# A decoder block with 32 experts on one core: gate and up products per matrix in four column groups, and another order at the end

## The chip, the cores and the metric

The kernel runs on 1 core of a Trainium2 chip. The metric is the device time of one execution in microseconds; the time before is 1613.85 us, the median of 3 runs (1612.68 to 1614.62).

## The reference, cut to what matters

One decoder layer over 256 tokens of width 2048, float32: RMS norm, an input projection, two attention branches (8 heads each), gates, an output projection; then a mixture of experts and a final RMS norm. The change lies in the experts and the end:

```
def hier_moe(h, ...):                      # 4 groups of 8 experts, 32 in all
    # each token: the best group, in it the two best experts, and their weights
    ...
    yb = (silu(xblk @ w_gate[e]) * (xblk @ w_up[e])) @ w_down[e]      # 2048 -> 512 -> 2048
    out[token] += yb * weight
x = x + hier_moe(rms_norm(x, norm2_g), ...)
return rms_norm(x, norm_f_g)
```

All 32 experts' matrices are read: 96 matrices of 2048 x 512 floats, 4.19 MB each.

## The kernel before

The first 680 us compute attention and projections. The routing then gives each expert up to 32 slots (`CAP`); four experts (a `QUAD`) share a tile of 128 slots. `gather` makes the quad's tokens, transposed, with one-hot products into `xq`. `hidden(e)` multiplies: for each of 16 slices k of the 2048 inputs the 32 slots are the stationary operand (128 x 32) and a row of the matrix is the moving one. The array is used as four column groups of 32 columns, `c` = 0 to 3: two for the gate matrix and two for up, each with 256 of the 512 hidden columns. The hidden columns are dealt out so that `w_down` can be read in long rows: line 723 gives a group neighbouring pairs of floats, every other pair.

```
rhs = (gw, uw)[c // 2][j].rearrange("p (q a b) -> p a q b", a=2, b=2)[:, c % 2]
nc.tensor.matmul(gu[c * CAP:(c + 1) * CAP], lhsT, rhs, start=(k == 0), stop=(k == KT - 1))
```

A float32 product is one instruction in the listings of the program, and two weight loads with two matmuls in the trace. Gate and up go side by side: a slice k of gate, the same of up. After silu, product and two transposes (`hTe`), `expert` multiplies with the down matrix (four column groups of 512 outputs, `py`), copies to `y`, and after four experts `combine` adds the slots to the tokens' rows `x1` with a product with the weighted one-hot matrix `owT` (float32).

The matrices come through a ring of five slots of 4.19 MB (`W`, `G`, `H`, `Q`, `O`), filled by SyncE's queue in the order of `plan`; a transfer is issued when its slot's last content has been used. At the start of the stage the slots hold gate, up, down 0, gate 1 and then up 1; expert 2's gate and up come in parts of 1 and 2 MB, each into the part of a slot that expert 0 has just used (line 398 and on). From down 2 (the name for expert 2's down matrix) on, whole matrices follow in the order gate, up, down.

At the end gate 31 and up 31 come in halves and quarters and are multiplied side by side, with `keep_clock` products (line 546, results unused) between the quarters. Down 31 comes in five column blocks, `BLOCKS`, on SyncE's queue; block by block: `last_down`, a copy, `combine` with `owl`, the squares for the norm. `norm_out` scales and writes eight blocks on SyncE's queue. The order of instructions on each engine is set by a scheduler that goes by data dependences and its own estimates, so it differs in places from the order of the code.

Of the kernel before, what the change touches and what calls it, by code (L numbers as in the profile page):

```python
# [9 lines left out]
F32 = mybir.dt.float32  # L10
F32R = mybir.dt.float32r
# [3 lines left out]
OP = mybir.AluOpType  # L15
# [17 lines left out]
BIG = 1e30  # L33
CH = 512
ROUTING_WAIT = 4
LOAD_WAIT = 2
BLOCKS = ((0, 512), (512, 512), (1024, 512), (1536, 256), (1792, 256))


@with_exitstack  # L40
def decoder_block(ctx, tc, x, g1T, w_in, b_gates, w_out_m, w_out_d, w_o, g2T, g2r, wr, br,
# [25 lines left out]
    def at(shape, name="at"):  # L67
        return psum.tile(shape, F32, tag="at", name=name, bufs=2)
# [336 lines left out]
    tags = [again[(len(rest) + i) % 5] for i in range(4)]  # L405
    for lo, hi in ((0, 8), (8, 12), (12, 16)):
        plan += [(kind, NE - 1, lo, hi, tags[i], lo) for i, kind in enumerate("gu")]
    plan_at = [0]

    def ring_part():  # L410
# [296 lines left out]
            k = k0 + j  # L707
            nc.scalar.activation(out=xq[:, k // 8, k % 8], in_=p[:, j], func=AF.Copy, scale=g2p[:, k:k + 1])

    def hidden(e, og=None):  # L710
        s0 = (e % QUAD) * CAP
        gu = at([P, S], name="gu")
        if og:
            gather(og, 0)
            gather(og, 2)
        for half in range(2):
            gw = units("g", e, 8 * half, 8 * half + 8)
            uw = units("u", e, 8 * half, 8 * half + 8)
            for j in range(8):
                k = 8 * half + j  # L720
                lhsT = xq[:, half, j, s0:s0 + CAP]
                for c in range(4):
                    rhs = (gw, uw)[c // 2][j].rearrange("p (q a b) -> p a q b", a=2, b=2)[:, c % 2]
                    nc.tensor.matmul(gu[c * CAP:(c + 1) * CAP], lhsT, rhs, start=(k == 0), stop=(k == KT - 1))  # L724
                if og and j % 4 == 3 and k + 1 < KT:
                    gather(og, k + 1)
                    gather(og, k + 3)
                if e == NE - 1 and j % 4 == 3 and k + 1 < KT:
                    keep_clock(LOAD_WAIT, rows[0][0][:, 0:4])
        sil = t2([P, S], name="sil")  # L730
        nc.scalar.activation(out=sil[64:128], in_=gu[0:64], func=AF.Silu)  # L731
        hh = t2([P, S], name="hh")
        nc.vector.tensor_tensor(out=hh[64:128], in0=gu[64:128], in1=sil[64:128], op=OP.mult)  # L733
        ph = tp([P, 2, 64])
        hv = hh[64:128].rearrange("q (p j) -> q j p", j=2)
        for j in range(2):
            nc.tensor.transpose(ph[:, j], hv[:, j], ident[64:128, 64:128])
        hTe = t2([P, 2, 2, CAP], name="hTe")
        nc.vector.tensor_copy(out=hTe, in_=ph.rearrange("p j (a s) -> p j a s", a=2))  # L739
        return hTe  # L740

    def expert(e, y, og):
        s0 = (e % QUAD) * CAP
        hTe = hidden(e, og)
# [12 lines left out]
        for c in range(4):
            src, dst = py[c * CAP:(c + 1) * CAP], y[c][s0:s0 + CAP]
            if c % 2:
                nc.vector.tensor_copy(out=dst, in_=src)  # L760
            else:
                nc.scalar.copy(out=dst, in_=src)  # L762

    def combine(owT, yc, b0, w):
        cs = slice(b0, b0 + w)
        for t in range(NT):
            p = acc([P, CH], name="pc")[:, 0:w]
            nc.tensor.matmul(p, owT[:, t * P:(t + 1) * P], yc, start=True, stop=True)
            nc.vector.tensor_tensor(out=x1[:, t, cs], in0=p, in1=x1[:, t, cs], op=OP.add)

    for q in range(NQ):
        if q:
            og = onehots(q, False, "og")
        owT = None
        y = []
        for e in range(q * QUAD, (q + 1) * QUAD):
            if e < NE - 1:
                expert(e, y, og if e % QUAD == 0 else None)
            if e % QUAD == 0:
                ows = onehots(q, True, "ow")  # L780
                owT = slots_T(ows)
                if q == NQ - 1:

                    last = []
                    for t in range(NT):
                        o = t2([P, QUAD, CAP], name="ol")
                        nc.vector.tensor_copy(out=o, in_=ows[t][:, P - CAP:].unsqueeze(1).to_broadcast([P, QUAD, CAP]))
                        last.append(o.rearrange("p e s -> p (e s)"))
                    owl = slots_T(last)
            if e == 1:  # L790
                keep_rows()
            if e == min(NE - 2, (q + 1) * QUAD - 1):
                for c in range(4):
                    combine(owT, y[c], c * CH, CH)

    hTe = hidden(NE - 1)
    gfs, gfr = (slot(tags[2])[:, i * D:(i + 1) * D] for i in range(2))
    nc.sync.dma_start(gfr[0:1], gf)
    last_slot = slot(tags[3])
    last_view = w_down[NE - 1].rearrange("(p j) c -> p j c", j=4)  # L800
    last_dw = []
    for b0, w in BLOCKS:
        t = last_slot[:, 4 * b0:4 * (b0 + w)].rearrange("p (j c) -> p j c", j=4)
        nc.sync.dma_start(t, last_view[:, :, b0:b0 + w])
        last_dw.append(t)
    nc.gpsimd.partition_broadcast(gfs, gfr[0:1])
    sf = region("bgs", [P, NT, len(BLOCKS)], name="sf")
    nc.scalar.activation(out=warm, in_=hTe[:, 0, 0, 0:1], func=AF.Sqrt, scale=0.0, bias=one)

    def last_down(b):  # L810
        w = BLOCKS[b][1]
        dw = last_dw[b]
        py = acc([P, CH], name="py")[:, 0:w]
        for i in range(4):
            nc.tensor.matmul(py[i * CAP:(i + 1) * CAP], hTe[:, i % 2, i // 2], dw[:, i],
                             start=True, stop=True)
        yl = t2([P, CH], name="yl")[:, 0:w]
        if b < len(BLOCKS) - 1:
            nc.scalar.copy(out=yl, in_=py)
        else:  # L820
            nc.vector.tensor_copy(out=yl, in_=py)
        return yl

    def square_sums(b):
        b0, w = BLOCKS[b]
        cs = slice(b0, b0 + w)
        for t in range(NT):
            sq = t2([P, CH], name="sq")[:, 0:w]
# [8 lines left out]
    def norm_out():  # L837
        rfs = []
        n = len(BLOCKS) - 1
        most = sm([P, NT], name="most")  # L840
        nc.vector.tensor_reduce(out=most, in_=sf[:, :, 0:n], axis=AX.X, op=OP.add)
        nc.vector.tensor_scalar(most, most, 1.0 / D, EPS, op0=OP.mult, op1=OP.add)
        for t in range(NT):
            mf = sm([P, 1], name="mf")
            nc.scalar.activation(out=mf, in_=sf[:, t, n:n + 1], func=AF.Sqrt, scale=1.0 / D, bias=most[:, t:t + 1])
            rf = sm([P, 1], name="rf")
            nc.vector.reciprocal(rf, mf)
            rfs.append(rf)
        for t in range(NT):
            rf = rfs[t]  # L850
            for c in range(4):
                cs = slice(c * CH, (c + 1) * CH)
                if c == 3:
                    nc.vector.scalar_tensor_tensor(out=xg[t][:, cs], in0=x1[:, t, cs], scalar=rf, in1=gfs[:, cs],
                                                   op0=OP.mult, op1=OP.mult)
                elif t == 0:
                    nc.vector.tensor_scalar(xg[t][:, cs], xg[t][:, cs], rf, None, op0=OP.mult)
                else:
                    nc.scalar.activation(out=xg[t][:, cs], in_=xg[t][:, cs], func=AF.Copy, scale=rf)
                nc.sync.dma_start(out[t * P:(t + 1) * P, cs], xg[t][:, cs])  # L860
# [105 lines left out]
```

## Time and profile before

| | us |
|---|---|
| median of 3 runs | 1613.85 |
| the profiled execution | 1615.2 |
| its span | 1613.5 |
| TensorE busy (matmul) | 1275.5 |
| VectorE busy | 570.9 |
| ScalarE busy | 482.8 |

528.3 MB move in all, 327 GB/s over the span. The profile's clock figure is the share of TensorE's full clock that was granted: 0.891 over the whole. Line numbers are those of the kernel before, unless they stand in the change. "DMA share" is the mean busy share of the core's 16 DMA engines. In the chain of the execution that ended last, TensorE has 59% and DMA 36%, of which 35% is waiting for up matrices. "PEld" is a weight load of TensorE, "PE" a matmul.

### The profile page before, as it was taken

What the parts mean: (1) busy time and instruction counts of PE and PEld (TensorE: products, weight loads), DVE (VectorE), ACT (ScalarE), POOL (GpSimd) and SP (SyncE); (2) the same over time, 40 slices, a digit from 0 to 9 for tenths busy, and PEclk for the clock granted to TensorE, in tenths of its full rate; (3) what the DMA queues carried; (4) which work ended last, traced back from release to release, by engine and by line L of the source; (5) the groups of instructions that cost most, each with busy time, mean ns of one, the idle gap of its engine ahead of it and who ended that gap; (6) DMA issues with size and microseconds to landing.
All of it is one profiled execution on the core that took longest, in us unless ns stands there. A gap on an engine that the chain in (4) does not pass through costs nothing.

```text
span 1613.5 us, 22882 instructions
## 1 busy us (share of the span) xinstructions
PE 1275.5 (79%) x9531; PEld 875.1 (54%) x9532; DVE 570.9 (35%) x1078; ACT 482.8 (30%) x1004; POOL 132.3 (8%) x159
## 2 busy tenths in 40 slices
PE   8999999999999999995846755666656757647666
PEld 7888888888888878762422322322323323314322
DVE  5766666666666665511200200201102112102122
ACT  6555555565656554420100100101100101001003
POOL 0200001013223130001000000000000000000001
PEclk9999999999999999997968877878877878877878
DMA  8544454485545578699999999999999999999994
GB/s 288 191 160 172 160 206 157 157 317 205 201 166 207 193 239 283 239 378 430 430 429 432 431 431 430 430 432 428 431 430 434 431 430 428 430 432 431 432 417 150
DMA packets 82002, 528.30 MB, mean 327 GB/s; under 512 B 4706, under 2 KB 5986, under 8 KB 66914
## 3 DMA queue, kind: packets, MB, share of 16 engines
q1 hardware_dynamic: 80882, 526.41, 80.8%
q8 instruction: 77, 1.26, 0.3%
q10 hardware_dynamic: 1008, 0.35, 0.1%
q14 instruction: 35, 0.28, 0.0%
HBM read 524.65 MB, written 2.10 MB: 326 GB/s over the span
## 4 chain that ended last, share of the span: by engine, by line
PE 59%; DMA 36%; DVE 2%; ACT 1%; issue 1%; POOL 0%; SPq 0%; ACTq 0%; DVEq 0%
DMA ew<-in_w_up 35%; PE gu L724 11%; PE qk L260 7%; PE g L260 7%; PE py L750 4%; PE g L261 4%; PE qk L261 4%; PE y L260 4%; PE tp L705 2%; PE y L261 2%; PE v L153 2%; PE v L151 2%; PE v L152 2%; PE o L152 1%; PE o L153 1%; PE o L151 1%
## 5 line engine op out<-in xcount | busy, mean ns | idle before, releaser
L724 PE MATMUL gu<-ew,xq 128*32 128x256 f32 x4096 | 311.7, 446 | 262.2 <-DMA ew<-in_w_up 185.0
L724 PEld LDWEIGHTS gu<-ew,xq 128*32 128x32 f32 x4096 | 152.1, 123 | 423.9 <-DMA ew<-in_w_up 200.8
L128 DVE TENSOR_TENSOR S<-raw,S 128x512 fp32r<-128x512 f32 x410 | 303.3, 749 | 192.4 <-ACT S L127 165.2
L127 ACT ACTIVATE S<-raw 128x512 fp32r<-128x512 f32 x410 | 257.6, 631 | 229.2 <-DVE S L128 74.0
L733 DVE TENSOR_TENSOR hh<-gu,sil 64x256 f32<-64x256 f32 x32 | 13.7, 427 | 572.7 <-ACT sil L731 572.7
L260 PE MATMUL qk<-hT,S 128*128 128x512 f32 x512 | 185.8, 406 | 0.0
L260 PE MATMUL g<-hT,S 128*128 128x512 f32 x512 | 181.8, 399 | 0.0
L731 ACT ACTIVATE sil<-gu 64x256 f32<-64x256 f32 x32 | 12.0, 376 | 519.6 <-PE gu L724 519.6
L261 PE MATMUL g<-hT,S 128*128 128x256 f32 x512 | 143.7, 281 | 0.0
L261 PE MATMUL qk<-hT,S 128*128 128x256 f32 x512 | 143.0, 280 | 0.0
L750 PE MATMUL py<-ew,hTe 128*32 128x512 f32 x976 | 121.7, 643 | 5.7 <-DVE hTe L739 5.7
L260 PEld LDWEIGHTS g<-hT,S 128*128 128x128 f32 x512 | 96.2, 188 | 23.4
L260 PEld LDWEIGHTS qk<-hT,S 128*128 128x128 f32 x512 | 96.8, 190 | 21.7 <-DVE hT L169 0.2
L760 DVE COPY y<-py 32x512 f32<-32x512 f32 x62 | 42.7, 689 | 168.6 <-ACT y L762 168.3
L261 PEld LDWEIGHTS qk<-hT,S 128*128 128x128 f32 x512 | 97.2, 190 | 0.8
L261 PEld LDWEIGHTS g<-hT,S 128*128 128x128 f32 x512 | 96.6, 189 | 0.1
L762 ACT COPY y<-py 32x512 f32<-32x512 f32 x62 | 35.7, 576 | 187.3 <-PE py L750 168.5
L260 PE MATMUL y<-oT,S 128*128 128x512 f32 x256 | 90.3, 398 | 0.3 <-ACT S L127 0.3
L261 PE MATMUL y<-oT,S 128*128 128x256 f32 x256 | 71.4, 281 | 0.1
L750 PEld LDWEIGHTS py<-ew,hTe 128*32 128x32 f32 x976 | 30.3, 118 | 74.8 <-issue 65.8
L705 PEld LDWEIGHTS tp<-og,x1p 128*128 128x128 f32 x448 | 58.6, 206 | 21.2 <-issue 13.5
L705 PE MATMUL tp<-og,x1p 128*128 128x128 f32 x448 | 63.2, 299 | 7.9 <-ACT og L640 6.7
(221 smaller groups left out, 1383.0 us busy)
## 6 DMA issues: line engine op xcount, KB each, us to landing
ew<-in_w_gate SPq DMA_DIRECT2D x29, 4096.0 KB, 39.2
ew<-in_w_up SPq DMA_DIRECT2D x29, 4096.0 KB, 42.7
ew<-in_w_down SPq DMA_DIRECT2D x29, 4096.0 KB, 29.8
raw<-in_w_in SPq DMA_DIRECT2D x38, 2048.0 KB, 7.8
ew<-in_w_gate SPq DMA_DIRECT2D x10, 1024.0 KB, 8.5
S2s<-in_w_o SPq DMA_DIRECT2D x38, 256.0 KB, 5.2
ew<-in_w_down SPq DMA_DIRECT2D x9, 1024.0 KB, 7.4
raw<-in_w_out_m SPq DMA_DIRECT2D x4, 2048.0 KB, 8.5
```

The costliest lines, as they stand in the source:

```text
L127: a = nc.scalar.activation(out=hi, in_=raw, func=AF.Copy)
L128: b = nc.vector.tensor_tensor(out=lo, in0=raw, in1=hi.bitcast(F32), op=OP.subtract)
L151: nc.tensor.matmul(a[t], lhs_hi[:, ts_], hi, start=(k == 0), stop=False)
L152: nc.tensor.matmul(a[t], lhs_hi[:, ts_], lo, start=False, stop=False)
L153: nc.tensor.matmul(a[t], lhs_lo[:, ts_], hi, start=False, stop=(k == nk - 1))
L260: nc.tensor.matmul(a[i], hi[:, bs], h2, start=(kk == 0), stop=False)
L261: nc.tensor.matmul(a[i][:, 0], lo[:, bs], h2[:, 0], start=False, stop=(kk == nk - 1))
L705: nc.tensor.matmul(p[:, j], rows[0][t][:, k0 + j], og[t], start=(t == 0), stop=(t == NT - 1))
L724: nc.tensor.matmul(gu[c * CAP:(c + 1) * CAP], lhsT, rhs, start=(k == 0), stop=(k == KT - 1))
L750: nc.tensor.matmul(py[c * CAP:(c + 1) * CAP], hTe[:, j % 2, j // 2], dw[c], start=(j == 0), stop=(j == 3))
L760: nc.vector.tensor_copy(out=dst, in_=src)
L762: nc.scalar.copy(out=dst, in_=src)
```

## The change

Gate and up get a PSUM tile each. Each matrix is multiplied in four column groups of 128 hidden columns, so an expert has 16 x 4 x 2 = 128 products of 128 columns where it had 64 of 256; a group's columns are every fourth float. All of gate comes before up, except in the first expert of a quad, where four slices of each alternate. Silu and product now work on 128 rows x 128 columns, with one transpose. At the end the order of transfers and products is gate 30, up 30, gate 31, down 30, up 31, down 31. Experts 30 and 31 have one-hot matrices of their own, not weighted (`of_one`); their outputs are scaled by the slot weights and split into a rounded part and a rest (`weighted`), and summed with two float32r products. Down 31's first block goes on ScalarE's queue, the rest in two loads on SyncE's; the output is written in four transfers on both queues.

```diff
-LOAD_WAIT = 2
-BLOCKS = ((0, 512), (512, 512), (1024, 512), (1536, 256), (1792, 256))
+LOAD_WAIT = 5
+BLOCKS = ((1536, 512), (0, 512), (512, 512), (1024, 256), (1280, 256))
+LAST_LOADS = ((1536, 512), (0, 1024), (1024, 512))
...
-    rest = [("d", 2)] + [(kind, e) for e in range(3, NE - 1) for kind in "gud"]
+    rest = [("d", 2)] + [(kind, e) for e in range(3, NE - 2) for kind in "gud"]
+    rest += [("g", NE - 2), ("u", NE - 2), ("g", NE - 1), ("d", NE - 2), ("u", NE - 1)]
...
+    def quarters(kind, e, og=None):
+        s0 = (e % QUAD) * CAP
+        p = at([P, P], name="gu")
+        def steps(k0, k1):
+            w = units(kind, e, k0, k1)
+            for k in range(k0, k1):
+                rhs = w[k - k0].rearrange("p (q c) -> p c q", c=4)
+                for c in range(4):
+                    nc.tensor.matmul(p[c * CAP:(c + 1) * CAP], xq[:, k // 8, k % 8, s0:s0 + CAP], rhs[:, c],
+                                     start=(k == 0), stop=(k == KT - 1))
+        return p, steps
...
+        if og:
+            for k in range(0, KT, 4):
+                gather(og, k)
+                gather(og, k + 2)
+                g_steps(k, k + 4)
+                u_steps(k, k + 4)
+        else:
+            g_steps(0, KT)
+            u_steps(0, KT)
...
+    def weighted(p, col, name):
+        w = p.shape[1]
+        hi, lo = (t2([P, CH], F32R, name=name)[:, 0:w] for _ in range(2))
+        nc.scalar.activation(out=hi, in_=p, func=AF.Copy, scale=slot_w[:, col:col + 1])
+        nc.vector.scalar_tensor_tensor(out=lo, in0=p, scalar=slot_w[:, col:col + 1], in1=hi.bitcast(F32),
+                                       op0=OP.mult, op1=OP.subtract)
+        return hi, lo
...
+    ohT30, ohT31 = of_one(NE - 2, 0), of_one(NE - 1, 1)
+    hT30 = hidden(NE - 2)
+    load_last(nc.scalar, *LAST_LOADS[0])
+    (g31, g_steps), (u31, u_steps) = (quarters(kind, NE - 1) for kind in "gu")
+    g_steps(0, KT)
+    keep_clock(LOAD_WAIT, rows[0][0][:, 0:4])
+    y30 = weighted(products(NE - 2, hT30), 0, "y30")
...
+    keep_clock(LOAD_WAIT, rows[0][0][:, 0:4])
+    u_steps(0, KT)
+    gfs, gfr = (slot(tags[1])[:, i * D:(i + 1) * D] for i in range(2))
     nc.sync.dma_start(gfr[0:1], gf)
+    for b0, w in LAST_LOADS[1:]:
+        load_last(nc.sync, b0, w)
+    hTe = activated(g31, u31)
...
+        for t in range(NT):
+            p = acc([P, CH], name="pc")[:, 0:w]
+            for i in range(2):
+                nc.tensor.matmul(p, ohT31[:, t * P:(t + 1) * P], yl[i], start=(i == 0), stop=(i == 1))
+            add_block(p, t, slice(b0, b0 + w))
```

Where the scheduler puts the products, on TensorE at the start of the expert stage, from the third quarter of expert 0 to expert 2. Before (`gu` are gate and up products, L705 gathers, L737 transposes, `py` down products):

```order
L724 MATMUL gu<-ew,xq 32x256 x16
L705 MATMUL tp<-og,x_4910 128x128 x8
L724 MATMUL gu<-ew,xq 32x256 x33
L737 MATMUL tp<-ident,hh 128x64 x2
L724 MATMUL gu<-ew,xq 32x256 x4
L750 MATMUL py<-ew,hTe 32x512 x16
L684 MATMUL tp<-ident,ow 128x128 x2
L724 MATMUL gu<-ew,xq 32x256 x45
L737 MATMUL tp<-ident,hh 128x64 x2
L750 MATMUL py<-ews,hTe 32x512 x8
L750 MATMUL py<-ew,hTe 32x512 x8
L724 MATMUL gu<-ew,xq 32x256 x62
```

After, the same stretch:

```order
L720 MATMUL gu<-ew,xq 32x128 x32
L705 MATMUL tp<-og,x_4910 128x128 x8
L720 MATMUL gu<-ew,xq 32x128 x37
L731 MATMUL tp<-ident,hh 128x128
L720 MATMUL gu<-ew,xq 32x128 x8
L755 MATMUL py<-ew,hTe 32x512 x16
L684 MATMUL tp<-ident,ow 128x128 x2
L720 MATMUL gu<-ew,xq 32x128 x120
L731 MATMUL tp<-ident,hh 128x128
L720 MATMUL gu<-ew,xq 32x128 x8
L755 MATMUL py<-ews,hTe 32x512 x8
L755 MATMUL py<-ew,hTe 32x512 x8
```

In both a few of the next expert's products are drawn ahead of the transposes, and the order of the pieces is the same. What moved is within a piece: an expert's 64 products are 128 of half the width, gate before up.

On TensorE at the end, before, from expert 30's transposes on (`idle` are the keep-clock products, `pc` the slot sums):

```order
L737 MATMUL tp<-ident,hh 128x64 x2
L750 MATMUL py<-ew,hTe 32x512 x16
L768 MATMUL pc<-y,owT 128x512 x8
L724 MATMUL gu<-ew,xq 32x256 x2
L546 MATMUL idle<-x1p,ident 128x512 x2
L724 MATMUL gu<-ew,xq 32x256 x30
L546 MATMUL idle<-x1p,ident 128x512 x2
L724 MATMUL gu<-ew,xq 32x256 x16
L546 MATMUL idle<-x1p,ident 128x512 x2
L724 MATMUL gu<-ew,xq 32x256 x16
L737 MATMUL tp<-ident,hh 128x64 x2
L815 MATMUL py<-ew,hTe 32x512 x8
```

After, from down 29 on; the first keep-clock call has been moved up, around gate 30:

```order
L755 MATMUL py<-ew,hTe 32x512 x16
L777 MATMUL pc<-y,owT 128x512 x8
L546 MATMUL idle<-x1p,ident 128x512 x2
L720 MATMUL gu<-ew,xq 32x128 x64
L546 MATMUL idle<-x1p,ident 128x512 x3
L720 MATMUL gu<-ew,xq 32x128 x64
L731 MATMUL tp<-ident,hh 128x128
L720 MATMUL gu<-ew,xq 32x128 x64
L755 MATMUL py<-ew,hTe 32x512 x16
L848 MATMUL pc<-y_11702,ohT 128x512 x4
```

And the end of it, from the last slot sums of expert 30, with the second keep-clock call whole and up 31 behind it:

```order
L848 MATMUL pc<-y_11702,ohT 128x512
L848 MATMUL pc<-y_11703,ohT 128x512
L546 MATMUL idle<-x1p,ident 128x512 x5
L720 MATMUL gu<-ew,xq 32x128 x64
L731 MATMUL tp<-ident,hh 128x128
L867 MATMUL py<-ew,hTe 32x512 x8
L918 MATMUL pc<-yl,ohT 128x512 x4
```

Down 29 and its sums now stand ahead of all of gate 30, up 30 and gate 31; only up 31 is left behind expert 30's sums.

## Rows read from the trace of the kernel before

**Rows 1.** Page: instructions of each engine; 40 slices of 40 us each.
```profile
PE 1275.5 (79%) x9531; PEld 875.1 (54%) x9532; DVE 570.9 (35%) x1078; ACT 482.8 (30%) x1004; POOL 132.3 (8%) x159
...
DMA  8544454485545578699999999999999999999994
...
GB/s 288 191 160 172 160 206 157 157 317 205 201 166 207 193 239 283 239 378 430 430 429 432 431 431 430 430 432 428 431 430 434 431 430 428 430 432 431 432 417 150
```

**Rows 2.** Stretches: us, busy (x count) by engine, clock, DMA share, GB/s.
```profile
700.00:720.00 20.00, 20.00 (x246) 11.70 (x249) 3.42 (x9) 4.70 (x10) 0.00 (x0) 1.00 0.98 385
...
1400.00:1500.00 100.00, 66.36 (x690) 34.56 (x690) 12.42 (x23) 10.00 (x26) 2.08 (x4) 0.79 1.00 431
...
1548.00:1558.00 10.00, 9.79 (x123) 5.20 (x124) 0.00 (x0) 0.00 (x0) 0.00 (x0) 0.70 0.98 418
...
1572.00:1586.00 14.00, 13.73 (x140) 5.98 (x136) 0.42 (x1) 0.19 (x1) 0.00 (x0) 1.00 0.82 296
```

**Rows 3.** Timeline of SyncE's queue: start us, us, queue, line, transfer.
```profile
691.49 0.33 SPq L416 DMA_DIRECT2D ew<-in_w_down  x1
...
697.13 0.33 SPq L416 DMA_DIRECT2D ew<-in_w_down  x1
...
720.60 0.33 SPq L416 DMA_DIRECT2D ew<-in_w_down  x1
...
729.77 0.33 SPq L416 DMA_DIRECT2D ew<-in_w_up  x1
```

**Rows 4.** Timeline of TensorE, experts 0 to 2: gathers, products, down.
```profile
691.37 3.75 PE L705 MATMUL tp<-og,x 128*128 128x128 f32 x16
...
695.05 2.02 PE L724 MATMUL gu<-ew,xq 128*32 128x256 f32 x32
...
711.41 3.63 PE L750 MATMUL py<-ew,hTe 128*32 128x512 f32 x32
...
725.91 7.46 PE L724 MATMUL gu<-ew,xq 128*32 128x256 f32 x124
```

**Rows 5.** Weight loads that write tp: ns min/median/max, first and last start.
```profile
L705 PEld LDWEIGHTS tp<-og,x1p x448: 186/192/338, 766.0 to 1492.4; 128*128 128x128 f32 x150
...
L705 PEld LDWEIGHTS tp<-og,x x64: 291/311/313, 684.7 to 705.9; 128*128 128x128 f32 x64
...
L737 PEld LDWEIGHTS tp<-ident,hh x64: 191/202/216, 710.5 to 1586.8; 64*128 64x128 f32 x64
...
L684 PEld LDWEIGHTS tp<-ident,ow x16: 138/144/183, 715.0 to 1502.9; 128*128 128x128 f32 x16
```

**Rows 6.** Timeline of the tail, all engines.
```profile
1548.21 10.20 PE L724 MATMUL gu<-ew,xq 128*32 128x256 f32 x124 [9.38 <-DMA ew<-in_w_up]
...
1564.59 7.11 PE L768 MATMUL pc<-y,owT 128*128 128x512 f32 x16 [0.79 <-ACT y L762]
...
1572.20 1.98 PE L546 MATMUL idle<-x1p,ident 128*128 128x512 f32 x4
...
1585.81 0.38 ACT L731 ACTIVATE sil<-gu 64x256 f32<-64x256 f32 x1 [20.04 <-PE gu L724]
...
1587.18 0.29 DVE L739 COPY hTe<-tp 128x128 f32<-128x128 f32 x1 [0.54 <-PE tp L737]
...
1589.38 1.98 PE L768 MATMUL pc<-yl,owT 128*128 128x512 f32 x4
...
1590.55 0.69 DVE L769 TENSOR_TENSOR x<-pc,x 128x512 f32<-128x512 f32 x1 [3.07 <-PE pc L768]
...
1601.31 5.41 SPq L860 DMA_DIRECT2D out<-ew  x8
```

**Rows 7.** Page: DMA queues, the one that loads TensorE's instructions.
```profile
q8 instruction: 77, 1.26, 0.3%
```

**Rows 8.** Timeline of TensorE, two float32r products of 512 columns.
```profile
675.90 0.39 PE L151 MATMUL o<-S,gT 128*128 128x512 f32 x1
...
676.13 0.39 PE L152 MATMUL o<-S,gT 128*128 128x512 f32 x1
```

More of the change, by code (lines that the diff above doesn't have):

```diff
@@ L402, in decoder_block @@
     again = ("W", "G", "H", "Q", "O")
[L403 removed]
+    rest = [("d", 2)] + [(kind, e) for e in range(3, NE - 2) for kind in "gud"]
+    rest += [("g", NE - 2), ("u", NE - 2), ("g", NE - 1), ("d", NE - 2), ("u", NE - 1)]
     plan += [(kind, e, 0, UN, again[i % 5], 0) for i, (kind, e) in enumerate(rest)]
[L405 to L407 removed]
+    tags = [again[(len(rest) + i) % 5] for i in range(2)]
     plan_at = [0]
@@ L710, in hidden, with activated @@
+    def activated(g, u):
+        sil = t2([P, P], name="sil")
+        nc.scalar.activation(out=sil, in_=g, func=AF.Silu)
+        hh = t2([P, P], name="hh")
+        nc.vector.tensor_tensor(out=hh, in0=u, in1=sil, op=OP.mult)
+        ph = tp([P, P])
+        nc.tensor.transpose(ph, hh, ident)
+        hTe = t2([P, 4, CAP], name="hTe")
+        nc.vector.tensor_copy(out=hTe, in_=ph.rearrange("p (c s) -> p c s", c=4))
+        return hTe
     def hidden(e, og=None):
-        s0 = (e % QUAD) * CAP
@@ L712, in hidden @@
-        gu = at([P, S], name="gu")
+        (g, g_steps), (u, u_steps) = (quarters(kind, e) for kind in "gu")
         if og:
[L714 to L744, printed above, removed]
+            for k in range(0, KT, 4):
[6 more added lines that the diff above has]
+            u_steps(0, KT)
+        return activated(g, u)
+    def products(e, hTe):
         py = acc([P, CH], name="py")
@@ L749, in expert, with down @@
             for c in range(4):
-                nc.tensor.matmul(py[c * CAP:(c + 1) * CAP], hTe[:, j % 2, j // 2], dw[c],
-                                 start=(j == 0), stop=(j == 3))
+                nc.tensor.matmul(py[c * CAP:(c + 1) * CAP], hTe[:, j], dw[c], start=(j == 0), stop=(j == 3))
+        return py
+    def down(e, hTe, y):
+        s0 = (e % QUAD) * CAP
+        py = products(e, hTe)
         if not y:
@@ L769, in combine, with of_one, add_block @@
             nc.vector.tensor_tensor(out=x1[:, t, cs], in0=p, in1=x1[:, t, cs], op=OP.add)
+    def of_one(e, col):
+        wide = [P, QUAD, CAP]
+        ohT = reg.tile([P, S], F32R, tag="owT", name="ohT", bufs=2)
+        pT, pw = tp([P, S]), tp([P, 1])
+        for t in range(NT):
+            o, ow = t2(wide, name="oh"), t2(wide, name="ow")
+            nc.vector.tensor_tensor(out=o, in0=r1[:, t, e:e + 1].unsqueeze(2).to_broadcast(wide),
+                                    in1=asc.unsqueeze(1).to_broadcast(wide), op=OP.is_equal)
+            nc.vector.tensor_scalar(ow, o, wt[:, t, e:e + 1], None, op0=OP.mult)
+            nc.tensor.transpose(pT[:, t * P:(t + 1) * P], o.rearrange("p e s -> p (e s)"), ident)
+            nc.tensor.matmul(pw, ow.rearrange("p e s -> p (e s)"), one, start=(t == 0), stop=(t == NT - 1))
+        nc.vector.tensor_copy(out=ohT, in_=pT)
+        nc.vector.tensor_copy(out=slot_w[:, col:col + 1], in_=pw)
+        return ohT
+    def weighted(p, col, name):
[5 more added lines that the diff above has]
+        return hi, lo
+    def add_block(p, t, cs):
+        nc.vector.tensor_tensor(out=x1[:, t, cs], in0=p, in1=x1[:, t, cs], op=OP.add)
     for q in range(NQ):
@@ L775, in decoder_block @@
         y = []
-        for e in range(q * QUAD, (q + 1) * QUAD):
-            if e < NE - 1:
-                expert(e, y, og if e % QUAD == 0 else None)
+        own = range(q * QUAD, (q + 1) * QUAD if q < NQ - 1 else NE - 2)
+        for e in own:
+            down(e, hidden(e, og if e % QUAD == 0 else None), y)
             if e % QUAD == 0:
[L780 to L789, printed above, removed]
+                owT = slots_T(onehots(q, True, "ow"))
@@ L790, in decoder_block @@
             if e == 1:
                 keep_rows()
[L792 to L797, printed above, removed]
-    nc.sync.dma_start(gfr[0:1], gf)
[L799 to L805, printed above, removed]
+        for c in range(4):
+            combine(owT, y[c], c * CH, CH)
@@ new lines, in decoder_block, with load_last @@
+    slot_w = region("slot_w", [P, 2], name="slot_w")
+    ohT30, ohT31 = of_one(NE - 2, 0), of_one(NE - 1, 1)
+    hT30 = hidden(NE - 2)
+    last_slot = slot(tags[0])
+    last_view = w_down[NE - 1].rearrange("(p j) c -> p j c", j=4)
+    last_dw = [None] * len(BLOCKS)
+    def load_last(queue, b0, w):
+        t = last_slot[:, 4 * b0:4 * (b0 + w)].rearrange("p (j c) -> p j c", j=4)
+        queue.dma_start(t, last_view[:, :, b0:b0 + w])
+        for b, (c0, cw) in enumerate(BLOCKS):
+            if b0 <= c0 < b0 + w:
+                last_dw[b] = t[:, :, c0 - b0:c0 - b0 + cw]
@@ new lines, in decoder_block @@
+    load_last(nc.scalar, *LAST_LOADS[0])
[3 more added lines that the diff above has]
+    y30 = weighted(products(NE - 2, hT30), 0, "y30")
+    for t in range(NT):
+        ps = [acc([P, CH], name="pc") for _ in range(4)]
+        for i in range(2):
+            for c in range(4):
+                rs_ = slice(c * CAP, (c + 1) * CAP)
+                nc.tensor.matmul(ps[c], ohT30[rs_, t * P:(t + 1) * P], y30[i][rs_], start=(i == 0), stop=(i == 1))
+        for c in range(4):
+            add_block(ps[c], t, slice(c * CH, (c + 1) * CH))
@@ L814, in last_down @@
         for i in range(4):
[L815 to L822, printed above, removed]
+            nc.tensor.matmul(py[i * CAP:(i + 1) * CAP], hTe[:, i], dw[:, i], start=True, stop=True)
+        return weighted(py, 1, "yl")
     def square_sums(b):
```

38 lines of the change are left out of this document (21 added, 17 removed).

## The prediction

> **What bounds the kernel now.** I read the page's slices first. The DMA share is mostly four to six tenths until about 690 us; from there it is at its top, and the rate near 430 GB/s, until the last two slices [rows 1]. So the expert stage is a stream of 4.19 MB matrices, 4.19/0.431 = 9.73 us each (stretch 1400 to 1500 of [rows 2]), and TensorE waits for it; its clock falls to the lower level in those waits (mean 0.70 in 1548 to 1558, right after one). Work on TensorE costs nothing there as long as the slots of the ring come free in time. That leaves two places where TensorE sets the end. One is the start of the stage, 684 to 735: five slots are full, and SyncE sends the next transfer when TensorE has used one up. The issue times in [rows 3] follow TensorE's rows: 691.49 and 697.13 stand right behind quarters of expert 0 [rows 4], 729.77 behind half of expert 2's 7.46 us. The other is the tail: up 30 lands at 1548.2, and from there one chain of TensorE pieces runs to 1600 (gate and up 30, down 30, the slot sums at 1564.59, matrix 31 between keep-clock products, hTe at 1587.2) [rows 6]; the stream is dying out by then (share 0.82, 296 GB/s in 1572 to 1586) [rows 2].
>
> **The gate and up products.** A "pair" below is one weight load and one matmul of the trace. Before, an expert has 128 pairs of 256 columns in 7.46 us at full clock, a quarter of them 2.02 less the last one's own tail [rows 4]: 57 ns a pair, as four column groups run at once, 228 ns a group of four. The change makes 256 pairs of 128 columns of them. [...] But the moving operand changes its step too. Before it takes two neighbouring floats and skips two; now one and skips three. No row has such a matmul. The nearest rows are weight loads [rows 5]: 128 weights that lie 64 bytes apart (x) take 311 ns against 192 for the same load from packed rows (x1p); 128 that lie 8 bytes apart (hh) take 202 against 144 packed (ow). Reads that leave gaps are slower, by 58 and 119 ns. So I take it that 128 floats with gaps of three cost as many as 256 in twos, and keep 57 ns: 14.6 us an expert, 7.3 a matrix. Lower end 30 ns; upper end the whole 311 ns per group of four, 78 ns.
>
> [...]
>
> **Term 1, start of the stage: +11.5 us.** I write the issues forward with 57 ns. In expert 0 a quarter is 3.75 us of gathers [rows 4] plus 32 pairs (1.85) before, 64 pairs (3.65) after: 5.6 against 7.4 us. Each quarter frees two 1 MB parts, which take 2.1 MB at the 385 to 400 GB/s of that stretch (700 to 720 in [rows 2]), 5.3 us. Before, the DMA engines are just kept fed; after, the queue runs dry by 0.4, 2.15, 0.3, 2.15 and 0.2 us in the four quarters (two of the parts are freed in mid quarter): 5.2. Then down 2 waits for gate 1's slot. Before, it is issued at 720.60, when expert 1's products end [rows 3]; my ledger has the queue dry 2.0 us there. After, TensorE ends down 0 at 720.3 (3.63 us, as [rows 4] has it), gate 1 at 727.7; the queue has work to 725.5 and data flow again 1.9 us behind the issue: dry 4.1. Up 3 needs the first half of up 2: 727.7 + 7.3 (up 1) + 2 (hidden) + 3.6 (down 1) + 7.3 (gate 2) + 3.7 = 751.5, +1.9; gate 3 has landed at 749.1: dry 4.2, where before there was none (729.77 was early). 13.5 - 2.0 = 11.5. From then on an expert is 14.6 + 2 + 3.6 = 20.2 us of TensorE against 29.2 of stream, and a first expert of four adds 8 us of gathers and 7 of sums: no slot is late again, and nothing is made up either. The stream is 11.5 us late to the end. Ends: 30 ns gives -2.0 (gate 1's slot comes free before up 1 is used), 45 ns +2.9, 70 ns +20.5, 78 ns about +27.
>
> **Term 2, instructions: +1.2 us.** TensorE's code is loaded from HBM by queue q8, 1.26 MB for 19,063 instructions [rows 7], 66 bytes each. 8192 more are 0.54 MB of a full stream, 0.54/0.431 = 1.2 us.
>
> **Term 3, the tail: +5.4 us.** In the clock of the old stream (up 30 lands 1548.2, so up 29 at 1519.0, gate 30 at 1538.5, gate 31 at 1557.9; down 30 behind it plus the 1 MB that ScalarE's queue puts in between, 1570.1; up 31 1579.8; the last piece 1587). [...] No row has two loaded queues. The order of TensorE after: up 29 to 1526.3, the hidden chain (silu, product, transpose, copy; 1585.81 to 1587.47 before, and the wait for the products' end) +1.9; then the four one-hot products of 30 and 31 with eight VectorE steps and four copies between them, about 3.4 (an estimate at 0.29 a step, as hTe's copy); down 29 3.6, its copies 0.8 and the slot sums 7.1 [rows 6], to 1543; two keep-clock products 1.9 [rows 6]; gate 30 7.3; three more 2.6; up 30 to 1562; transpose 1.3; gate 31 to 1571; down 30 3.6; the scaled copies hi and lo 1.6; five of the eight adds (0.69 each) until the next PSUM bank is free, 1580.0; five keep-clock products 4.3; up 31 to 1591.6; hidden 1.7: hTe at 1593.3, against 1587.5 [rows 6]. +5.8. So TensorE, not the stream, sets this tail in my forecast, although gate 31 is done early.
>
> Behind hTe before: 26.0 us. A block's sums fall from 1.98 us (fp32) to four float32r products of 0.23, the spacing of the two rows in [rows 8], so TensorE saves about 1 us a block. VectorE takes over: five lo copies (3 x 0.7 + 2 x 0.45) more on top of the ten adds (5.9 us), 8.9 us in all from about 1.9 behind hTe, and each lo sits between a product and its add: the last add at about +11.8, where it was +12.2. The output goes in four transfers of 0.5 MB on two queues instead of eight whose issue alone took 5.41 us [rows 6], but the first is only ready after 1024 columns: I take it as even. Sum -0.4, between -2 and +1. [...]
>
> **Sum.** 11.5 + 1.2 + 5.4 = 18.1 on the profiled execution's 1615.2: 1633.3. The median of the runs lies 1.35 lower, so 1632.
>
> **Rivals.**
> A. The pair follows its columns (30 ns). For: at the lower clock the same pairs take longer (10.20 us for an expert that starts cold [rows 6] against 7.46), so the array and not the issue sets the 57. Against: [rows 5]. Term 1 is -2.0, term 2 stays; up 31 takes 3.8 us behind its landing at 1579.8, hTe at 1585.2 if TensorE is free by then, -2.3; behind it -0.4: -3.5, 1610.4, faster. If the five keep-clock products stand in front of up 31, hTe is at 1591 and the sum is +2, 1616. It is decided by the price: below some 36 ns, with the chain of adds done before 1580, the change wins.
> B. About 45 ns, an issue limit between the two. Term 1 +2.9, term 3 +4.0: +8, 1622. For it: nothing in the trace shows more pairs per us than 17.5 for long.
> C. 70 ns: +20.5, and five matrices of the tail chain 1.6 longer each: +35, 1649. For it: the four groups' reads might get in each other's way.
> D. 57 ns, but the start is covered (the parts are freed sooner than I write down): tail and code alone, +6.6, 1620. Against: the ledger gives the old issue times within 1.1 us.
>
> **Chances.** Forecast 0.56 (its own range 1626 to 1638), A 0.24 (0.14 below 1610.6, 0.10 about even), B 0.10, C 0.05, D 0.05. About 0.2%, 3.2 us, is what a measurement can tell from no change. Slower: 0.56 + 0.10 + 0.05 + 0.05 = 0.76; even 0.10; faster 0.14. The range that leaves out 0.2: 1611 to 1640.
>
> **What would show it.** A matmul group of 128 columns at 57 ns a pair and gate or up alone about 7.3 us; SyncE's issues of expert 2's parts 7.4 instead of 5.6 us apart, down 2 near 728 and up 3 near 751; a DMA share clearly below 0.98 in 700 to 760; hTe 17 to 19 us later than 1587.5. A pair near 30 ns, or issue times as before, makes the forecast wrong; so does hTe right behind the landing of up 31.

## The result, and the profile after

The changed kernel takes 1636.51 us (median of 4 runs, 1634.58 to 1637.56) against 1613.74 for the kernel before (4 runs, 1612.68 to 1614.62): a ratio of 1.0142, 95% interval 1.0127 to 1.0156, or 22.8 us slower. The profiled execution took 1636.71 us, its span is 1635.0, 21.5 longer than before.

The page of the changed kernel, the rows that answer to [rows 1]: engine busy times; slices of 41 us; and the queue that loads instructions ([rows 7]).

```profile
PE 1449.5 (89%) x13629; PEld 1055.4 (65%) x13630; DVE 574.0 (35%) x1098; ACT 478.8 (29%) x1002; POOL 132.3 (8%) x159
...
DMA  8544454485554668689999999999999999999992
GB/s 284 188 162 168 169 189 155 163 341 186 185 201 165 245 221 294 250 322 405 427 433 430 428 429 432 426 432 429 427 432 427 431 428 432 428 430 430 429 389 91
...
q8 instruction: 109, 1.79, 0.4%
```

TensorE is busy for 174 us more, and most of that is beside the stream. Where it counts shows in the slices: 322 and 405 GB/s at the start of the expert stage, where [rows 1] has 378 and 430. The same by stretches (columns as in [rows 2]):

```profile
680.00:700.00 20.00, 18.88 (x168) 13.76 (x171) 5.84 (x40) 5.01 (x15) 0.00 (x0) 1.00 0.94 387
700.00:720.00 20.00, 20.00 (x224) 14.34 (x219) 1.39 (x6) 4.06 (x10) 0.00 (x0) 1.00 0.82 301
720.00:740.00 20.00, 19.97 (x303) 11.45 (x299) 2.38 (x5) 1.44 (x3) 0.78 (x1) 1.00 0.89 362
740.00:760.00 20.00, 19.16 (x295) 12.02 (x291) 2.41 (x5) 2.01 (x4) 7.37 (x8) 1.00 0.90 371
...
1400.00:1500.00 100.00, 75.25 (x970) 44.90 (x971) 13.21 (x29) 9.60 (x24) 1.56 (x3) 0.91 1.00 430
```

From 700 to 760 the DMA share is 0.82 to 0.90 while TensorE is busy for 59 of the 60 us: the stream waits for TensorE there. Later the share is 1.00 again; in 1400 to 1500 TensorE is busy for 75 us where [rows 2] has 66, and its mean clock is 0.91 against 0.79.

TensorE at the start (answers to [rows 4]), and SyncE's issues ([rows 3]):

```profile
689.54 3.90 PE L720 MATMUL gu<-ew,xq 128*32 128x128 f32 x64
...
721.91 14.03 PE L720 MATMUL gu<-ew,xq 128*32 128x128 f32 x240
```
```profile
693.53 0.33 SPq L416 DMA_DIRECT2D ew<-in_w_down  x1
...
701.03 0.33 SPq L416 DMA_DIRECT2D ew<-in_w_down  x1
...
728.12 0.33 SPq L416 DMA_DIRECT2D ew<-in_w_down  x1
...
750.43 0.33 SPq L416 DMA_DIRECT2D ew<-in_w_up  x1
```

240 pairs in 14.03 us are 58.5 ns a pair. The first issues stand 7.5 us apart; down 2 goes out at 728.12 and up 3 at 750.43, where [rows 3] has 720.60 and 729.77.

The tail of the changed kernel (answers to [rows 6]), all engines:

```profile
1534.14 7.63 PE L720 MATMUL gu<-ew,xq 128*32 128x128 f32 x128 [2.34 <-DMA ew<-in_w_up]
...
1545.70 5.34 PE L755 MATMUL py<-ew,hTe 128*32 128x512 f32 x32
1551.82 7.10 PE L777 MATMUL pc<-y,owT 128*128 128x512 f32 x16 [0.79 <-ACT y L771]
...
1586.42 3.64 PE L755 MATMUL py<-ew,hTe 128*32 128x512 f32 x32
...
1592.94 3.01 PE L848 MATMUL pc<-y,ohT 32*128 32x512 f32 x8 [0.56 <-DVE x L806]
...
1595.88 7.20 PE L546 MATMUL idle<-x1p,ident 128*128 128x512 f32 x10
...
1603.00 7.63 PE L720 MATMUL gu<-ew,xq 128*32 128x128 f32 x128
...
1611.48 0.29 DVE L733 COPY hTe<-tp 128x128 f32<-128x128 f32 x1 [0.42 <-PE tp L731]
...
1625.11 0.39 SPq L900 DMA_DIRECT2D out<-ew  x1
...
1626.23 1.39 SPq L909 DMA_DIRECT2D out<-ew  x2
```

The row at 1534.14 is up 29; after it no row of TensorE's gate and up products waits for a transfer. Five keep-clock products, 7.20 us long, stand right ahead of up 31. hTe ends at 1611.77, 24.3 later than before.

### The profile page after: what moved, and what is told of

It reads as the page before. It is cut to its first block, busy times and chain, and to the rows that moved or that the text cites. A ratio compares the mean times of both kernels' runs of the same rounds, so it can differ in the third digit from the quotient of the medians.

```text
span 1635.0 us, 31113 instructions
## 1 busy us (share of the span) xinstructions
PE 1449.5 (89%) x13629; PEld 1055.4 (65%) x13630; DVE 574.0 (35%) x1098; ACT 478.8 (29%) x1002; POOL 132.3 (8%) x159
## 3 DMA queue, kind: packets, MB, share of 16 engines
q8 instruction: 109, 1.79, 0.4%
## 4 chain that ended last, share of the span: by engine, by line
PE 63%; DMA 33%; DVE 2%; ACT 1%; issue 1%; POOL 0%; SPq 0%; ACTq 0%; DVEq 0%
DMA ew<-in_w_up 19%; DMA ew<-in_w_down 12%; PE gu L720 12%; PE g L261 7%; PE qk L261 7%; PE py L755 4%; PE tp L705 4%; PE g L262 4%; PE qk L262 4%; PE y L261 4%; PE pc L777 3%; PE y L262 2%; PE v L152 2%; PE v L154 2%; PE v L153 2%; PE o L153 1%
## 5 line engine op out<-in xcount | busy, mean ns | idle before, releaser
L720 PE MATMUL gu<-ew,xq 128*32 128x128 f32 x8192 | 485.1, 409 | 113.8 <-DMA ew<-in_w_gate 69.3
L720 PEld LDWEIGHTS gu<-ew,xq 128*32 128x32 f32 x8192 | 334.3, 130 | 267.6 <-issue 140.6
L729 DVE TENSOR_TENSOR hh<-gu,sil 128x128 f32<-128x128 f32 x32 | 9.3, 292 | 556.8 <-PE gu L720 556.8
L755 PEld LDWEIGHTS py<-ew,hTe 128*32 128x32 f32 x976 | 34.0, 117 | 82.9 <-issue 68.2
L727 ACT ACTIVATE sil<-gu 128x128 f32<-128x128 f32 x32 | 8.9, 278 | 255.9 <-PE gu L720 255.9
L708 ACT ACTIVATE xq<-tp,g2p 128x128 f32<-128x128 f32 x128 | 40.1, 364 | 85.3 <-PE tp L705 85.1
L705 PEld LDWEIGHTS tp<-og,x1p 128*128 128x128 f32 x448 | 53.2, 191 | 17.9 <-issue 10.4
```

Of the source, the lines that this page charges most:

```text
L705: nc.tensor.matmul(p[:, j], rows[0][t][:, k0 + j], og[t], start=(t == 0), stop=(t == NT - 1))
L720: nc.tensor.matmul(p[c * CAP:(c + 1) * CAP], xq[:, k // 8, k % 8, s0:s0 + CAP], rhs[:, c], start=(k == 0), stop=(k == KT - 1))
L755: nc.tensor.matmul(py[c * CAP:(c + 1) * CAP], hTe[:, j], dw[c], start=(j == 0), stop=(j == 3))
```

## Experiments

Times are medians, and the ratio in brackets is to the kernel before on the same chip. That one took 1614.96 us beside the kernels with neighbours, with every second float, with old products in experts 0 to 2 and with no keep-clock products; 1614.84 beside the two without keep-clock products and with every second float, the new output and the first mixed kernel; 1614.23 beside the other three. The changed kernel's 1636.51 us stand beside 1613.74, so a difference from it is good to about 1 us.

### Neighbouring floats for a column group, and every second float

```diff
-rhs = w[k - k0].rearrange("p (q c) -> p c q", c=4)            # changed kernel: every 4th
+rhs = w[k - k0].rearrange("p (c q) -> p c q", c=4)            # neighbours
+rhs = w[k - k0].rearrange("p (h q b) -> p h b q", h=2, b=2)   # or every 2nd of half a row
...                                                             # down matrices read to match
```

> The changed kernel, but a column group takes 128 neighbouring floats of a matrix row instead of every fourth float (the down matrices are read with their rows dealt out to match, in pieces of 8 KB). Theory stride (the step of the moving operand sets the 57 to 59 ns of a pair): a pair falls to 30 to 36 ns, a gate or up matrix alone to 3.9 to 4.6 us, up 3 is issued at 727 to 731 instead of 750.4, and the time falls by 14 to 20 us, to about 1619 (13.5 us of start, 3 to 6 of tail; the keep-clock products stay). Rival issue limit (a pair of 128 columns costs 57 ns however its floats lie, four groups take turns at issue): pair 57 to 59 ns, issues and time as in the changed kernel, 1636.

> The changed kernel, but a column group takes every second float of half a row (two floats used of each four in a row, as before the change, at 128 columns a product); the down matrices are dealt out to match. Theory stride, by lines of 16 bytes: the same price as neighbouring floats, 30 to 36 ns a pair, time about 1619. Theory stride, by distance (each further float costs): between, 40 to 50 ns, 1622 to 1628. Rival issue limit: 57 to 59 ns, 1636.

Measured: 1628.31 us with neighbours (1.0086, 95% interval 1.0070 to 1.0103) and 1623.02 with every second float (1.0052, 1.0035 to 1.0069). A run of 240 pairs on TensorE, neighbours and then every second float:

```profile
713.17 6.76 PE L723 MATMUL gu<-ew,xq 128*32 128x128 f32 x240
```
```profile
713.30 7.14 PE L731 MATMUL gu<-ew,xq 128*32 128x128 f32 x240
```

28.2 and 29.8 ns a pair, with up 3 issued at 730.3 and 730.6. So the step sets the price and no issue limit does; two used floats of each four are nearly as good as neighbours. Of the 17 us that I expected back, 8.2 and 13.5 came; the second time lies in the range given for a price by distance, although the price itself is the one by lines. By the profiled executions up 11 lands 10.6 and 11.4 us earlier than in the changed kernel, where 13.5 had been expected, and from up 27's landing to hTe it takes 1.4 and 4.1 us less, where 3 to 6 had been. The stream loses some of it again: with neighbours the down matrices come in 8 KB pieces, and from up 11's landing to up 27's it takes 477.8 us (475.2 with pieces of 16 KB, 474.0 in the changed kernel, 471.0 before).

### A step of eight floats

```diff
+rhs = two[kind, e, k - k % 2].rearrange("p (q c) -> p c q", c=8)[:, 4 * (k % 2):4 * (k % 2) + 4]
```

> The changed kernel with a step of eight floats instead of four in gate and up (each product takes every eighth float of two rows of a matrix; it leaves out a right sum: the rows are mixed, only the time counts). Theory lines (what costs is that each float of the moving operand lies in a 16-byte line of its own): 57 to 60 ns a pair, time as the changed kernel, 1634 to 1639. Rival distance (the cost goes on growing with the step): 100 ns a pair or more, an expert 26 us and above, time over 1660.

One execution took 1638.38 us. The same run of 240 pairs:

```profile
721.59 14.21 PE L723 MATMUL gu<-ew,xq 128*32 128x128 f32 x240
```

59.2 ns: a step of eight costs about what one of four does (58.5). The price has two levels here, near 29 ns where two or more floats of each 16 bytes are used, near 59 where one is.

### Old products in experts 0 to 2

```diff
     def hidden(e, og=None):
+        if e < 3:
+            return hidden_old(e, og)      # 256 columns, gate and up side by side
```

> The changed kernel, but experts 0 to 2 use the gate and up products of before (two groups each of 256 columns, side by side). Theory start (term 1): SyncE's issues come at the times of before (down 2 near 721, up 3 near 731), the stream is 10 to 12 us ahead from there to the end, time 1624 to 1627. Rival covered start (the lateness is made up later, or the tail alone costs the 23 us): time 1634 to 1637.

Measured: 1625.50 us (1.0065, 1.0048 to 1.0082), 11.0 less than the changed kernel, or 12.4 by the two ratios to the kernel before. Down 2 is issued at 719.50 and up 3 at 728.66. The start alone is worth about what term 1 said.

### No keep-clock products

```diff
-    keep_clock(LOAD_WAIT, rows[0][0][:, 0:4])     # both calls at the end
```

> The changed kernel without its ten keep-clock products at the end. Theory tail by TensorE (up 31 has landed some 8 us before its products start, five keep-clock products of 7.2 us stand right ahead of them): hTe comes 7 to 11 us sooner, time 1626 to 1630. Rival clock (without them the clock falls and the products of up 31 take 10 us and more): a gain of 0 to 4 us, 1633 to 1637, or a loss.

Measured: 1626.51 us (1.0073, 1.0056 to 1.0090), 10.0 less. TensorE's row for up 31:

```profile
1591.97 7.53 PE L720 MATMUL gu<-ew,xq 128*32 128x128 f32 x128 [0.84 <-DMA ew<-in_w_up]
```

It waits 0.84 us for the transfer, so up 31 had landed some 9 us before its products began in the changed kernel (up 29 lands 2.2 us earlier in this run, which brings 1591.97 to about 1594 there): the keep-clock products only stood in the way. The clock did fall without them (0.70 in 1585 to 1592), and yet up 31 took 7.53 us; the last section comes back to that.

### Every second float, without keep-clock products, on two queues and on one

The second kernel against the first:

```diff
-    load_last(nc.scalar, *LAST_LOADS[0])
...
-    for b0, w in LAST_LOADS[1:]:
+    for b0, w in LAST_LOADS:                      # all on SyncE
         load_last(nc.sync, b0, w)
```

> The kernel with every second float of half a row (1623.0 us) without its ten keep-clock products. There five of them (6.26 us, at a low clock) stand between expert 30's sums, done at 1586.4, and up 31, which by the landing of gate 31 (1563.7) plus two matrices and 1 MB is there at about 1585.5. Theory tail by TensorE: hTe 3.5 us (products of up 31 at the low clock, 6.5 us) to 6 us (full clock) sooner, 1617 to 1619.5. Rival clock (what the keep-clock products cost they give back): 1622 to 1624.

> The one without keep-clock products, with all of the last down matrix on SyncE's queue behind up 31 (no transfer on ScalarE's queue). Theory shared engines (a second queue's megabyte pushes the rest back): down 30 and up 31 land 2.4 us sooner, and with them hTe, 1.5 to 2.5 us less than the kernel with two queues, 1615 to 1617.5. Rival own bandwidth (the second queue's megabyte comes beside the first's): the same time or slower by up to 2 us, since its block then comes last.

Measured: 1619.27 us (1.0030, 1.0018 to 1.0042), and with one queue 1618.08 (1.0019, 1.0010 to 1.0028). The first came as expected, with up 31 in 5.44 us (the last experiment shows 3.84 at a granted clock of 1.00 and 6.42 at 0.57). The second gained 1.2 us where 1.5 to 2.5 were expected, so neither range holds it, and the intervals of the two kernels overlap. In the profiled executions the time from up 27's landing to down 30's is 110.85 us with two queues and 109.13 with one, and to up 31's 121.31 and 118.85: by then the megabyte on ScalarE's queue has held the other one up by 2.5 us, about the 2.4 that it takes at the stream's rate. Up 31 then took 6.42 us with one queue instead of 5.44, which gives 1.0 of it back.

### The kernel before with the new output only

```diff
-                nc.sync.dma_start(out[t * P:(t + 1) * P, cs], xg[t][:, cs])     # 8 x 0.25 MB
+                nc.sync.dma_start(rows_out[:, half], xg[t][:, half])            # t = 1: nc.scalar
...
+            nc.sync.dma_start(rows_out[:, 2 * CH:], xg[t][:, 2 * CH:])           # 4 x 0.5 MB
```

> The kernel before, with only the output changed: four transfers of 0.5 MB on two queues, with their scaling in that order, instead of eight of 0.25 MB on SyncE's queue. Theory output (the changed kernel has 23.2 us behind hTe where there were 26.0; of these 2.8 some 2.3 lie between the first issue of the output and the end): 1.5 to 2.5 us faster than before. Rival sums (the gain is from the float32r sums and the order of blocks): the same as before within 0.5 us.

Measured: 1612.40 us (0.9985, 0.9976 to 0.9994), 2.4 less than before. SyncE's output issues:

```profile
1601.57 0.38 SPq L854 DMA_DIRECT2D out<-ew  x1
1602.69 1.39 SPq L863 DMA_DIRECT2D out<-ew  x2
```

The first goes out when it did, the last is issued by 1604.08 instead of 1606.72 ([rows 6]: 1601.31 and 5.41 us of issue). That is as much as the changed kernel gains between its first issue of output and its end (2.3 us).

### The kernel before with its products cut in two

```diff
-nc.tensor.matmul(gu[c * CAP:(c + 1) * CAP], lhsT, rhs, start=(k == 0), stop=(k == KT - 1))
+for v in range(2):
+    nc.tensor.matmul(gu[c * CAP:(c + 1) * CAP, v * P:(v + 1) * P], lhsT, rhs[:, 64 * v:64 * v + 64], ...)
```

> The kernel before, with each gate and up product of 256 columns cut into two of 128 (same floats, same order of use, gate and up side by side): as many TensorE instructions as in the changed kernel, and nothing else of it. Theory columns (a pair of 128 columns with two floats used in each four costs half of one with 256): 30 ns a pair, an expert 7.7 us, SyncE's issues at the start as before. Theory code (term 2: the instructions themselves cost the stream the 3 us that the changed kernel loses between 1100 and 1360): up 27 lands at 1462 to 1464 instead of 1459.9, time 2 to 4 us above the kernel before, 1617 to 1619. Rival order (the 3 us come from the order in which slots are freed): the time of before within 0.7 us.

Measured: 1623.22 us (1.0055, 1.0041 to 1.0069), 9.0 more than before. The instructions themselves cost, and more than I expected. Two waits from the chain that ended last, the landing of up 11 and of up 27 (start and length), of the kernel before, the changed kernel and this one:

```profile
946.27 42.66 DMA ew<-in_w_up
...
1415.33 44.57 DMA ew<-in_w_up
```
```profile
957.14 43.13 DMA ew<-in_w_up
...
1427.99 46.26 DMA ew<-in_w_up
```
```profile
948.88 41.71 DMA ew<-in_w_up
...
1426.52 38.07 DMA ew<-in_w_up
```

Between the two landings lie 470.97, 473.98 and 474.00 us. The order of use is that of before in the last one, and its stream loses the same 3.0 us. The other 4.3 of its span's 7.3 us lie ahead of up 11 (1.7, of which 0.4 is a later first gather), between up 27 and up 30 (0.7) and in the tail (1.9), where TensorE also stood still without a wait that the profile names (last section). Pairs take 31 ns (244 in 7.55 us).

### Old products in 0 to 29, the new end with every second float, and keep-clock products where TensorE waits

```diff
     def hidden(e, og=None):
+        if e < NE - 2:
+            return hidden_old(e, og)
...
+    with tc.issue_after(last_step[0]):            # second kernel only, behind gate 31
+        keep_warm(8)
```

> Gate and up products of before (256 columns, side by side, down matrices as before) in experts 0 to 29; the new order of the end with every second float in 30 and 31, no keep-clock products, the last matrix on one queue. Theory code (the 3 us that the stream of the changed kernel loses between 1100 and 1360 beyond its late start come from TensorE's instructions, 8192 fewer here than there but for 512): the stream stands where it did before, up 27 lands at about 1460 (before 1459.9, changed 1474.3), hTe at 1584 to 1588 (before 1587.5), behind it 23.2, time 1608 to 1613. Rival (the 3 us have another cause, they stay): up 27 at 1463, time 1611 to 1616.

> The mixed kernel (1612.2 us) with keep-clock products where TensorE waits anyway: eight between gate 31 and down 30 (it waited 4.92 us there for down 30), and some between expert 30's sums, none ahead of up 31. Theory clock (down 30 in 4.99 us and up 31 in 6.42 us stood at the low clock): down 30 3.7, up 31 3.9, hTe 2 to 4 us sooner, 1608 to 1610.5. Rival in the way (the products run past the landing of down 30 or the sums, or the clock falls all the same): 1611.5 to 1614.

Measured: 1612.17 us (0.9984, 0.9975 to 0.9993) for the first, 1612.39 (0.9992, 0.9983 to 1.0001) for the second. The two waits again, in the first:

```profile
944.77 42.60 DMA ew<-in_w_up
...
1414.09 44.21 DMA ew<-in_w_up
```

Up 11 and up 27 land at 987.37 and 1458.30, 470.93 us apart, with 23 packets of TensorE's instructions between them (23 before, 39 in the changed kernel and in the one with cut products): without those instructions the 3 us are gone. This kernel is faster than both, by 2.7 us against the one before, and about as much as the new output alone gives. In the second, which also has keep-clock products between expert 30's sums, TensorE behind gate 31:

```profile
1562.86 7.13 PE L726 MATMUL warm<-x1p,ident 128*128 128x512 f32 x16
1569.92 3.64 PE L807 MATMUL py<-ew,hTe 128*32 128x512 f32 x32
...
1579.78 3.84 PE L738 MATMUL gu<-ew,xq 128*32 128x128 f32 x128
```

Down 30 and up 31 take 3.64 and 3.84 us, as the clock theory said (the granted clock is 1.00 from 1566 to 1585; in the first kernel they take 4.99 at 0.72 and 6.42 at 0.57). But the eight keep-clock products took 7.13 us, about what the 0.43 us a pair of the row of four in [rows 6] gives for their 16, where TensorE had waited 4.92 us in the first kernel, and down 30 started 3 us later than there. Both theories were half right, the time lies in the rival's range, and nothing is gained.

## Why the prediction was right, and where its terms were off

By its own steps, from the profiled executions (us):

| step | forecast | measured | read from |
|---|---|---|---|
| the run's own start | 0 | 1.2 | first gathers at 685.85, before 684.69 |
| term 1, start of the stage | 11.5 | 10.2 | up 11 lands 11.34 later, less 1.16 |
| term 2, instructions | 1.2 | 3.0 | up 27 lands 14.35 later |
| term 3, tail up to hTe | 5.8 | 9.9 | hTe 24.30 later, less 14.35 |
| behind hTe | -0.4 | -2.8 | 23.2 against 26.0 |
| sum | 18.1 | 21.5 | spans 1635.0 and 1613.5 |

**The pair.** "I keep 57 ns" for 128 floats with gaps of three: 58.5. Rivals A, B and C fell with it. The reason given holds too, as the experiments with neighbours, every second and every eighth float show. The number was a choice between 30 and 78, though, not a sum, and one of its two supports was weak: hh's 202 ns were set against ow's 144, while the packed load of x1p takes 192 in [rows 5]. The 30 ns of the lower end and of rival A were an estimate, near half of the old pair's 57; products of 128 columns took 28.2, 29.8 and 31 ns a pair where two or more floats of each 16 bytes are used, and 58.5 and 59.2 where one is.

**Term 1.** The mechanism and its places came as forecast: issues 7.5 us apart, down 2 at 728.12 (727.7), up 3 at 750.43 (751.5), a DMA share below 0.98 in 700 to 760. Old products in three experts of 32 took 11.0 us back. Rival D, a covered start, is out. Wait by wait the ledger was too dear: by the packets' times the DMA engines stand idle for 8.8 us in 690 to 765, and for 1.4 before, where it had 13.5 and 2.0. It lets data flow again 1.9 us behind an issue; no run shows that term, and here the first packets follow the issues at 728.12 and 750.43 after 1.0 us. Part of what remains of the 10.2 shows as a lower rate while data flow (353 GB/s at a share of 0.89 in 690 to 765, 404 at 0.99 before); the rest is not traced. So it is in part luck that 10.2 came so near to 11.5. The first gathers began 1.2 us later than before; the start of that stretch is not touched by the change, and over the other profiled executions it lies between 683.7 and 685.4.

**Term 2.** Right in kind, too small. The page shows what q8 moved (1.26 MB before, 1.79 after); that it comes from HBM no view shows. Counting the 0.54 MB at the stream's full rate gives 1.2 us; between up 11 and up 27 alone 3.0 are lost, in two kernels with these instructions that use the matrices in different orders, and none in the mixed kernel without them. That the instructions cost it is shown; that it is their loading is not. Why 16 more packets of 16 KB in that stretch go with 3.0 us, and not the 0.6 of their bytes, is open. One piece can be seen: between the two landings 202.4 MB come in on the stream's queue before, 202.3 in the mixed kernel, but 202.9 and 203.0 in the changed kernel and the one with cut products. Some 0.6 MB more, 1.4 us at the stream's rate, had thus gone to later matrices when up 27 was complete, as if some DMA engines had fallen behind others; the records don't say which engine moved a packet.

**Term 3.** TensorE sets this tail, as forecast, but two pieces were sized at full clock. Down 29 took 5.34 us where 3.6 stood in the sum (the granted clock was 0.66 in 1546 to 1551), and the five keep-clock products ahead of up 31 took 7.20 instead of 4.3 (0.63 in 1596 to 1603). These 4.6 are the whole difference of 4.1, and a little more. That ScalarE's megabyte pushes down 30 and up 31 back, which the sum counts at 2.4 us, no run before shows; with that megabyte behind up 31 on SyncE's queue the two landed 1.7 and 2.5 us sooner after up 27. The two stretches (columns as in [rows 2]):

```profile
1546.00:1551.00 5.00, 5.00 (x32) 1.13 (x24) 0.00 (x0) 0.00 (x0) 0.00 (x0) 0.66 1.00 426
...
1596.00:1603.00 7.00, 7.00 (x10) 2.67 (x10) 1.07 (x2) 0.00 (x0) 0.00 (x0) 0.63 0.43 166
```

Ahead of the first TensorE had run only transposes and products of one column for the slot weights since 1542, ahead of the second short slot sums that waited for VectorE's adds.

**Behind hTe.** "I take it as even", said of the output, is the step that failed. From hTe to the first issue of output the kernel saved 0.5 us (13.34 against 13.84), close to the -0.4; the output gave 2.3 more. The row for it was at hand: eight issues of 0.68 us each on one queue against three of 0.4 to 0.7 there and one on ScalarE's.

So the mechanism was right in kind in every term but the output. The total (1632 forecast, 1636.5 measured) is nearer than the terms because their misses partly cancel: 1.2, 1.8 and 4.1 us one way, 1.3 and 2.4 the other. That part is luck.

## What to carry to other kernels

Here the float32 matmuls of four column groups paid for the step of the moving operand: with two or more used floats in each 16 bytes 128 columns cost about half of 256 (28.2 to 31 ns a pair against 57), with one the same (58.5 and 59.2). Cutting products in two doubles their instructions, and in this kernel, where the stream of weights is the bound, these were not free: they cost the stream 3.0 us in 16 experts, and with pairs of 30 ns TensorE stood still for 13.9 to 27.8 us that no wait explains. Keep-clock products did harm ahead of data that had landed: without the ten the kernel took 10.0 us less. Count them at the clock that the pieces before them leave (five took 7.20 us at 0.63 where 4.3 had been counted), and even where TensorE waits against the wait's length: the eight behind gate 31, 7.13 us in a wait of 4.92, ran past the landing.

## What the runs showed that had not been expected

**The price with one float in four does not follow TensorE's clock.** Two stretches of the changed kernel that hold one matrix's 128 pairs each (columns as in [rows 2]):

```profile
882.50:890.00 7.50, 7.46 (x128) 4.97 (x128) 0.00 (x0) 0.00 (x0) 0.00 (x0) 1.00 0.98 417
...
1474.40:1482.00 7.60, 7.52 (x128) 5.06 (x128) 0.00 (x0) 0.00 (x0) 0.00 (x0) 0.78 1.01 433
```

7.46 and 7.52 us at clocks of 1.00 and 0.78. With neighbours 128 pairs follow the clock:

```profile
1550.97 3.70 PE L723 MATMUL gu<-ew,xq 128*32 128x128 f32 x128
...
1567.62 6.54 PE L723 MATMUL gu<-ew,xq 128*32 128x128 f32 x128 [5.73 <-DMA ew<-in_w_gate]
```

The second, right behind a wait, has a granted clock of 0.55. So what limits the products with gaps of three does not follow that clock; the reading of the operand would fit, but no run shows that it is this. It agrees with up 31's 7.53 us in the kernel without keep-clock products, at 0.84 in 1592 to 1600, against 7.63 with them. Rival A had taken the clock's effect on the old products (10.20 us at 0.71, 7.46 at 1.00) as a sign that the array sets their price; it says nothing of the new step.

**With short pairs TensorE seems to run out of instructions.** With pairs of 30 ns its gate and up products show idle time that the profile puts down to nothing ("issue"). The groups of the kernel before and of the one with products cut in two (busy, mean ns; idle before them, by what ended it):

```profile
L724 PE MATMUL gu<-ew,xq 128*32 128x256 f32 x4096 | 311.7, 446 | 262.2 <-DMA ew<-in_w_up 185.0 <-DMA ew<-in_w_gate 77.2
```
```profile
L725 PE MATMUL gu<-ew,xq 128*32 128x128 f32 x8192 | 316.6, 307 | 265.9 <-DMA ew<-in_w_up 174.5 <-DMA ew<-in_w_gate 63.4 <-issue 27.8
```

Two of its 22 stalls, at the start and in the tail:

```profile
736.31 0.61 PE L725 MATMUL gu<-ew,xq 128*32 128x128 f32 x4 [2.06 <-issue]
...
1564.35 0.68 PE L725 MATMUL gu<-ew,xq 128*32 128x128 f32 x14 [1.21 <-issue]
```

The last packets of the instruction queue before these two rows end at 734.99 and 1562.90, 1.3 and 1.45 us ahead. The same holds for all 22, and for the 12 stalls with neighbours and the 15 with every second float: each ends 1.2 to 1.6 us behind the end of a packet, though this kernel has only 109 of them in its 1621 us. That the stall ends with the arrival of code is read from this; no run took the fetch away. The kernel before has no such time, and the changed one, at 58 ns a pair, nearly none (1.4 us).

**The price of a down matrix read in shorter pieces.** With 32, 16 and 8 KB in a row for each partition the stretch from up 11 to up 27 took 474.0, 475.2 and 477.8 us, 16 down matrices of its 48: 0.08 and 0.24 us a matrix. The shorter pairs of these kernels are not the cause: with products cut in two the same stretch took 474.0.
